# Experts that gather rows normalised but not yet scaled, with the norm's factor and addend applied at the transposed columns

## The chip, the cores and the metric

The kernel runs on one core of one Trainium2 chip. The metric is the device time of one execution in microseconds. Engines are named as in the profile: PE multiplies matrices, PEld is PE's queue of weight loads, DVE, ACT and POOL do elementwise work, SP issues most DMA transfers.

## What is computed

One encoder layer over 512 tokens of width 1024: a token mixer (neighbourhood attention and a bidirectional gated delta rule), a layer norm, a mixture of experts with 4 groups of 8, and a second layer norm.

```python
x = layer_norm(DEEPNORM_ALPHA * x + mix, ln1_g, ln1_b)        # ((x - mean) * rsqrt(var + eps)) * g + b
group_p, group_idx = lax.top_k(softmax(xt @ w_router_group + b_router_group), 1)
...
top_l, top_i = lax.top_k(sel, 2)                              # two experts inside the group
top_p = softmax(top_l) * group_p
...
hg, hu = split(einsum('nd,edf->nef', xt, w_expert_gate_up), 2)
hid = silu(hg) * hu * combine[:, :, None]
y = einsum('nef,efd->nd', hid, w_expert_down)
x = layer_norm(DEEPNORM_ALPHA * x + y, ln2_g, ln2_b)
```

All 512 tokens pass the first norm; each then goes to two of 32 experts.

## The kernel before

The program has two parts. In the first (all that runs through `emit`, line 447 in the profile) instructions are recorded, and a planner orders them: it goes through the ready instructions with estimated costs, takes those with the longest chain behind them first, and `plan.prio` adds to or takes from that rank. The planner sees the first part alone. In the second part (`tc.manual_schedule`) instructions stand on their engines in the order in which the code is written.

The first part ends with the mixer's output projection, the first norm and the router. The output rows lie in `xn`, four tiles of 128 tokens by 1024. The router's logits are computed from rows not yet normalised and mended with mean and factor (`cg`, `lg`), with the norm's factor multiplied into the router's weights (`wgb`). Beside them the norm is applied to `xn` in place, tile by tile in halves of 512 columns: a scaling, the product with `ln1_g`, the sum with `ln1_b`. The table `NORM1` names the engine of each of these three steps (V is DVE, G is POOL, S is ACT). The finished rows are stored to `x1d` in HBM, from where later pairs gather them. On SP's queue these four stores stand among the loads of the first twenty expert weight units (`first`, units 10 to 19 here). DVE then finds each token's group and experts (`arg_first`), PE ranks the tokens of each expert (`rk`), and DVE makes `SL`, each token's slot, and from it `oh`, a one-hot matrix that picks the first two experts' tokens. 18 products into `warm` keep PE at work meanwhile. Behind that come the combining weights (`vals`), and a few small steps for experts with more than 64 tokens (`more`, `moreT`, `pre`, `base`, `sx`, `we`, `nw`), among them a PE transpose of `more` and a PE product of its copy `moreT`.

The second part goes over 16 pairs of experts and a last round for overflowing tokens. Pair 0's rows come from `xn` by a one-hot product straight into the transposed form `xT` (lines 1675 to 1681: 1024 columns as eight blocks of 128, tokens of the pair along the free axis). All later pairs are gathered from `x1d` by an indirect DMA into `xg` (`gather`), and `turn` transposes them on PE in two halves and copies each half to `xT` on ACT. For each pair `up` multiplies `xT` with the gate and up weights, `act` makes `hid`, `hidden` transposes it, `down` multiplies with the down weights, `split` rounds the result into two parts, and `combine` adds it to the kept rows `xn`, eight pieces per pair, one pair later. The letters of `REST` give the order behind `up`: a `act`, t `turn`, p the list of the pair after next (`prep`: four products with `vals` and two ACT copies into `ic`; then `follow` starts the gather), h `hidden`, c a piece of `combine`, k and d, e the tail. PE results of h and p go to two halves of one PSUM tile, `tp`.

Of the kernel before, what the change touches and what calls it, by code (L numbers as in the profile page):

```python
# [9 lines left out]
F32 = mybir.dt.float32  # L10
FR = mybir.dt.float32r
F16 = mybir.dt.float16
I32 = mybir.dt.int32
AF = mybir.ActivationFunctionType
OP = mybir.AluOpType
# [4 lines left out]
NT = 4  # L20
KC = 8
# [49 lines left out]
NU = 20  # L71
# [10 lines left out]
REST = "attpchcccccccdke"  # L82
REST0 = "ahdektctp"

NORM1 = "VGV VGV VGV VGV VVG VVG SGV SVG".split()
NORM2 = "VSGG QD QSGG QPS QSGV QSGV QPS QD A B A B".split()


# [389 lines left out]
def encoder_block(ctx, tc, aps, out):  # L478
# [683 lines left out]
    def first(u, place=None):  # L1162
        W[u] = place.tile([128, 4, 512], F32, name="wu") if place else [gm_tile(F32, "wu") for _ in range(4)]
        yield lambda: load(Y, u, W[u])
# [82 lines left out]
    cgp = pmm.tile([128, 2, 36], F32, name="mm")  # L1247
    for k in range(KC):
        PE.matmul(cgp, one, wgb[:, k], start=k == 0, stop=k == KC - 1)
    cg = cp.tile([128, 2, 36], F32, name="cg")  # L1250
    V.tensor_copy(cg[:, 0], cgp[:, 0])
    V.tensor_tensor(cg[:, 1], cgp[:, 1], rb, op=OP.add)
# [57 lines left out]
            plan.prio = 0.0  # L1310
    wcs.close()
    wx.close()
    wc = pool("wc", NU - 14)
    for u in range(10, NU):
        for f in first(u, wc if u < NU - 4 else None):
            f()

    cq = pool("cq", 1, stack=pc)

# [11 lines left out]
    for t in range(NT):  # L1331
        v = xn[:, t]
        plan.prio = 20.0 if t == 3 else 0.0
        mv, r = norm_stats(ct, v)
        nm = ct.tile([128, 1], F32, name="nm")
        V.tensor_scalar(nm, mv[:, 0:1], -1.0, None, op0=OP.mult)
        plan.prio = 0.0
        V.scalar_tensor_tensor(lg[:, t], cg[:, 0], nm, lgp[t // 3][:, t % 3], op0=OP.mult, op1=OP.add)
        V.scalar_tensor_tensor(lg[:, t], lg[:, t], r, cg[:, 1], op0=OP.mult, op1=OP.add)
        plan.prio = 0.0  # L1340
        if "S" in NORM1[2 * t] + NORM1[2 * t + 1]:
            G.tensor_tensor(nm, nm, r, op=OP.mult)
        for h in range(2):
            c = v[:, h * 512:h * 512 + 512]
            g_, b_ = ln1[:, 0, h * 512:h * 512 + 512], ln1[:, 1, h * 512:h * 512 + 512]
            m = NORM1[2 * t + h]
            if m[0] == "S":
                S.activation(c, c, AF.Identity, scale=r, bias=nm)
            else:
                V.tensor_scalar(c, c, mv[:, 0:1], r, op0=OP.subtract, op1=OP.mult)  # L1350
            (V if m[1] == "V" else G).tensor_tensor(c, c, g_, op=OP.mult)
            (V if m[2] == "V" else G).tensor_tensor(c, c, b_, op=OP.add)
    for t in range(NT):
        Y.dma_start(x1d[t * 128:t * 128 + 128], xn[:, t])


    desc = C2["desc"]
# [1 line left out]
    def one_hot(oh, sl):  # L1359

        sh = [128, NT, 2, 64]
        V.tensor_tensor(oh.rearrange("p t (a s) -> p t a s", a=2),
                        C2["iota"][:, None, None, 0:64].to_broadcast(sh),
                        sl.unsqueeze(3).to_broadcast(sh), op=OP.is_equal)
# [45 lines left out]
    for i in range(18):  # L1410
        PE.matmul(warm[:, i % 4], ident, ew, start=True, stop=True, skip_group_check=True)

    plan.prio = -20.0
    ge = cq.tile(g4, F32, name="ge")
    V.tensor_tensor(ge, gl, gm.unsqueeze(2).to_broadcast(g4), op=OP.subtract)
    S.activation(ge, ge, AF.Exp)
# [26 lines left out]
    V.tensor_tensor(vals[:, :, :, 1], Cf, vals[:, :, :, 0].bitcast(F32), op=OP.subtract)  # L1443
    V.tensor_tensor(vals[:, :, :, 2].rearrange("p t (g e) -> p t g e", e=8), tk, ogb, op=OP.mult)

    ni = cq.tile([128, 32], I32, name="ni")
    V.tensor_scalar(ni, rk[:, 4], 1.0, -1.0, op0=OP.max, op1=OP.add)
    V.tensor_scalar(ni, ni, 6, None, op0=OP.logical_shift_right)
# [4 lines left out]
    G.affine_select(out=tri, in_=tri, pattern=[[1, 32]], compare_op=OP.is_ge, fill=0.0, base=0, channel_multiplier=-1)  # L1453
    mt = ppc.tile([128, 4, 128], F32, name="x1tp", bufs=2)
    PE.transpose(mt[0:32, 0], more, ident)
    moreT = cq.tile([32, 128], F32, name="moreT")
    V.tensor_copy(moreT, mt[0:32, 0])
    PE.matmul(mt[:, 1, 0:32], moreT, tri[0:32], start=True, stop=True, skip_group_check=True)
    pre = cq.tile([128, 32], F32, name="pre")
# [1 line left out]
    base = cq.tile([128, 32], F32, name="base")  # L1461
    V.tensor_tensor(base, pre, more, op=OP.subtract)
    V.tensor_scalar(base, base, 64.0, -64.0, op0=OP.mult, op1=OP.add)
    sx = cq.tile(s32, F32, name="sx")
    V.tensor_tensor(sx, SL, base[:, None].to_broadcast(s32), op=OP.add)
    V.scalar_tensor_tensor(sx, SL, 2048.0 + 64, sx, op0=OP.is_ge, op1=OP.mult)
    sm = mo.tile([128, 2, NT], F32, name="sm")
# [6 lines left out]
    for i, c in enumerate((c1, c2)):  # L1474
        V.tensor_copy(vm[:, i, :, 0], c)
        V.tensor_copy(vm[:, i, :, 2], C2["tokinv"])
    we = cq.tile([1, 16, 32], F32, name="we")
    V.tensor_scalar(pre, pre, 2048.0, None, op0=OP.add)
    V.tensor_tensor(we, C2["iota"][0:1, 0:16].unsqueeze(2).to_broadcast([1, 16, 32]),
                    pre[0:1, None].to_broadcast([1, 16, 32]), op=OP.is_ge)  # L1480
# [16 lines left out]
    def pool(name, bufs=1, space=None, stack=ctx, side=None):  # L1497
        kw = {} if space is None else {"space": space}
        if side is not None:
            kw["side"] = side  # L1500
        return stack.enter_context(tc.tile_pool(name=name, bufs=bufs, reuse_waits="tile", **kw))

    W = {u: [x.real() for x in w] if isinstance(w, list) else w.real() for u, w in W.items()}
    vals, SL, oh, nw, xn, sm, vm = [x.real() for x in (vals, SL, oh, nw, xn, sm, vm)]
    ident, magic = ident.real(), magic.real()
    C2 = {k: v.real() for k, v in C2.items()}
    ue = ExitStack()
# [41 lines left out]
        tc.chain_iter_dep(f"load{u % 2}", getattr(op[0], "ins", op[0]))  # L1549

    part = ep_.tile([128, 4, 512], FR, name="part", bufs=1)
    hot = ep_.tile([128, 512], FR, name="hot", bufs=1)
    xT = ep_.tile([128, KC, 128], F32, name="xT", bufs=1)
    xg = [ep_.tile([128, D], F32, name=f"xg{i}", bufs=1) for i in range(2)]
    for x in xg:
        G.memset(x, 0.0)
# [1 line left out]
    def turn(src, i, dst):  # L1558

        tp = pg.tile([128, 4, 128], F32, name="gat")  # L1560
        for k in range(4):
            PE.transpose(tp[:, k], src[:, (4 * i + k) * 128:(4 * i + k) * 128 + 128], ident)
        S.copy(dst[:, 4 * i:4 * i + 4], tp)

    def prep(ic, oh, e, ip):

        for t in range(NT):
            PE.matmul(ip[:, 0:6], oh[:, t], vals[:, t, e:e + 2].rearrange("p a b -> p (a b)"), start=t == 0,
                      stop=t == NT - 1, skip_group_check=True)
        for a in range(2):  # L1570
            S.copy(ic[rows2[a]], ip[rows2[a], 3 * a:3 * a + 3])  # L1571
# [53 lines left out]
    def small(j):  # L1625
        ic[j] = ep_.tile([128, 3], F32, name="ic", bufs=3)
        ix[j] = ep_.tile([128, 1], I32, name="ix", bufs=3)
        cw[j] = ep_.tile([128, 1], F32, name="cw", bufs=3)

    def follow(j, dst):  # L1630

        number(ic[j], ix[j])
        G.tensor_tensor(cw[j], ic[j][:, 0:1], ic[j][:, 1:2], op=OP.add)  # L1633
        if dst is not None:
            gather(ix[j], dst)
# [35 lines left out]
    with tc.manual_schedule():  # L1671
        experts = windows_experts()
        oh1 = hot.rearrange("p (t s) -> p t s", t=NT)
        one_hot(oh1, SL[:, :, 2:4])
        for i in range(2):
            gp_ = pg.tile([128, 4, 128], F32, name="gat")
            for k in range(4):
                for t in range(NT):
                    PE.matmul(gp_[:, k], xn[:, t, (4 * i + k) * 128:(4 * i + k) * 128 + 128], oh[:, t].bitcast(F32),
                              start=t == 0, stop=t == NT - 1, skip_group_check=True)  # L1680
            (S.copy if i == 0 else V.tensor_copy)(xT[:, 4 * i:4 * i + 4], gp_)
            if i == 0:
                ip = pu.tile([128, 2, 256], F32, name="tp", bufs=1)
                for j, o in ((1, oh1), (0, oh)):
                    small(j)
                    prep(ic[j], o, 2 * j, ip[:, 1, 8 * j:8 * j + 6])
                    follow(j, xg[1] if j else None)
        for j in range(NP + 1):
            here, there = xg[j % 2], xg[(j + 1) % 2]
            hp, tpi, yps, hid = tiles()  # L1690
# [265 lines left out]
```

## Time and profile before

| | |
|---|---|
| median of three runs | 911.08 us (908.28 to 913.6) |
| the profiled execution | 910.17 us, of it 908.5 us from first to last instruction |
| PE busy | 857.5 us (94%) |
| PEld busy | 598.8 us (66%) |
| DVE busy | 520.2 us (57%) |
| POOL busy | 363.6 us (40%) |
| ACT busy | 354.0 us (39%) |
| mean granted TensorE clock | 0.975 |

Busy shares are means over stages that have different limits. The mixer runs to about 575 us, the norm and the router to 605, the experts to about 882, the second norm to the end. A row of the timeline gives start, duration, engine, line, operation, output<-inputs, shapes and count; a square bracket at its end gives how long the engine had been idle and what released it. Instructions that the planner ordered all have line 447 and are told apart by their tiles. Rows of several instructions run from the start of the first to the end of the last.

### The profile page before, as it was taken

To read this page: it belongs to the slowest core of one execution; us is meant where nothing else is said; L and a number is where in the kernel's file an instruction comes from. 1 tells how busy PE (TensorE), PEld (TensorE's weight loads), DVE (VectorE), ACT (ScalarE), POOL (GpSimd) and SP (SyncE) were. 2 spreads that over 40 slices of the span, in tenths; PEclk is the share of its full clock that TensorE was granted. 3 is DMA by queue.
4 is the path that set the end of the run, shared out by engine and by line. 5 is a ranking of instruction groups with operands and counts; after the bars stand their busy time and mean duration, and the time that the engine had idled before them with its cause. 6 is when DMAs were issued, how large, how long until landed. Compare 5 with 4: busy or idle time off the path is not lost. (4 is left out here: it accounts for less than half of the span.)

```text
span 908.5 us, 15388 instructions
## 1 busy us (share of the span) xinstructions
PE 857.5 (94%) x5667; PEld 598.8 (66%) x5667; DVE 520.2 (57%) x1181; ACT 354.0 (39%) x925; POOL 363.6 (40%) x500
## 2 busy tenths in 40 slices
PE   7999999999999998999999999778999999999984
PEld 5786677778767777778788899754454444544441
DVE  6787889642526483831523537844556464564648
ACT  5465555542666765542443331102121111212114
POOL 5766567547737463636557741411010010100003
PEclk9998999999999997999999999799999999999997
DMA  6221101111312111011347275959998999998922
GB/s 246 89 85 47 48 24 48 48 47 48 113 40 76 48 54 47 2 48 47 93 184 280 81 264 206 361 225 349 393 357 309 333 363 340 353 384 308 371 93 93
DMA packets 39966, 157.72 MB, mean 174 GB/s; under 512 B 5786, under 2 KB 6042, under 8 KB 29008
## 3 DMA queue, kind: packets, MB, share of 16 engines
q1 hardware_dynamic: 37584, 152.81, 46.4%
q0 software_dynamic: 2304, 3.90, 1.2%
q8 instruction: 45, 0.74, 0.3%
q14 instruction: 33, 0.27, 0.1%
HBM read 156.99 MB, written 4.19 MB: 177 GB/s over the span
## 5 line engine op out<-in xcount | busy, mean ns | idle before, releaser
L447 POOL TENSOR_TENSOR wlo<-wraw,whi 128x256 fp32r<-128x256 f32 (+1 forms) x220 | 165.6, 766 | 148.0 <-ACT whi L447 108.6
L447 PE MATMUL mm<-xhi,whi 128*128 128x512 f32 (+1 forms) x360 | 140.2, 416 | 7.7 <-ACT whi L447 4.8
L447 PE MATMUL mm<-xhi,wlo 128*128 128x512 f32 (+1 forms) x360 | 139.2, 411 | 0.0
L447 PE MATMUL mm<-xlo,whi 128*128 128x512 f32 (+1 forms) x360 | 138.0, 410 | 0.2 <-DVE xlo L447 0.2
L447 ACT CAST whi<-wraw 128x256 fp32r<-128x256 f32 (+1 forms) x228 | 88.1, 404 | 118.0 <-PE mm L447 73.5
L1647 PE MATMUL hp<-wu,xT 128*64 128x512 f32 x544 | 119.7, 592 | 0.0
L1633 POOL TENSOR_TENSOR cw<-ic 128x1 f32<-128x1 f32 x17 | 3.2, 186 | 220.5 <-ACT ic L1571 205.1
L1647 PEld LDWEIGHTS hp<-wu,xT 128*64 128x64 f32 x544 | 38.9, 137 | 76.7 <-issue 74.8
L447 PEld LDWEIGHTS mm<-xhi,whi 128*128 128x128 f32 (+1 forms) x360 | 67.7, 190 | 24.3 <-ACT whi L447 5.1
L1621 DVE TENSOR_TENSOR xn<-xn,gat 128x512 f32<-128x512 f32 x128 | 79.2, 681 | 3.9 <-PE gat L1619 3.9
L447 PEld LDWEIGHTS mm<-xlo,whi 128*128 128x128 f32 (+1 forms) x360 | 67.7, 190 | 12.1 <-DVE xlo L447 1.1
L447 PEld LDWEIGHTS mm<-xhi,wlo 128*128 128x128 f32 (+1 forms) x360 | 67.4, 190 | 11.1 <-POOL wlo L447 0.2
L1619 PE MATMUL gat<-part,hot 128*128 128x512 f32 x256 | 67.0, 404 | 0.0
L1668 PE MATMUL yp<-wu,hid 128*64 128x512 f32 x272 | 62.1, 598 | 0.5 <-ACT hid L1662 0.5
L1654 DVE SCALAR_TENSOR_TENSOR hid<-hid,hp 128x256 f32<-128x256 f32 x17 | 7.2, 421 | 91.9 <-ACT hid L1653 91.9
L1611 ACT CAST part<-yp 128x512 fp32r<-128x512 f32 x34 | 19.8, 586 | 95.2 <-PE yp L1668 94.0
L447 DVE TENSOR_TENSOR RR<-RR,ps 128x512 f16<-128x512 f16 x64 | 42.8, 682 | 17.6 <-PE ps L447 17.4
L1619 PEld LDWEIGHTS gat<-part,hot 128*128 128x128 f32 x256 | 45.4, 189 | 9.4 <-issue 0.8
L1653 ACT ACTIVATE hid<-hp 128x256 f32<-128x256 f32 x17 | 6.5, 384 | 110.2 <-PE hp L1647 110.2
L1668 PEld LDWEIGHTS yp<-wu,hid 128*64 128x64 f32 x272 | 18.0, 136 | 35.6 <-issue 34.9
L447 DVE TENSOR_TENSOR ylv<-ps,mlv 128x256 f16<-128x256 f32 x64 | 26.2, 419 | 18.8 <-PE ps L447 18.3
L447 PEld LDWEIGHTS <-RR 128*128 128x128 f16 x448 | 23.6, 100 | 16.2 <-issue 13.4
(375 smaller groups left out, 1763.0 us busy)
## 6 DMA issues: line engine op xcount, KB each, us to landing
wu<-in_wgu SPq DMA_DIRECT2D x54, 1024.0 KB, 6.6
wu<-in_wdn SPq DMA_DIRECT2D x28, 1024.0 KB, 6.7
wraw<-in_wT SPq DMA_DIRECT2D x42, 512.0 KB, 3.4
wu<-in_wgu SPq DMA_DIRECT2D x56, 256.0 KB, 5.7
wu<-in_wdn SPq DMA_DIRECT2D x24, 256.0 KB, 4.6
wraw<-in_wp SPq DMA_DIRECT2D x8, 512.0 KB, 3.7
wraw<-in_wo SPq DMA_DIRECT2D x8, 512.0 KB, 4.0
kqv<-in_rpb SPq DMA_DIRECT2D x4, 640.0 KB, 3.9
```

The costliest lines, as they stand in the source:

```text
L447: getattr(self.eng[o.eng], o.call)(*[f(v) for v in o.args], **{k: f(v) for k, v in o.kw.items()})
L1611: S.copy(part[:, c], yps[c])
L1619: PE.matmul(sm_, hot[:, t * 128:t * 128 + 128], part[:, 2 * i + h], start=i == 0, stop=i == 1)
L1621: V.tensor_tensor(v, v, sm_, op=OP.add)
L1633: G.tensor_tensor(cw[j], ic[j][:, 0:1], ic[j][:, 1:2], op=OP.add)
L1647: PE.matmul(hp[rows2[h]], xT[:, k, rows2[h]], gw(j, h, k), start=k == 0, stop=k == KC - 1, skip_group_check=True)
L1653: S.activation(hid, hp[:, 0:256], AF.Tanh, scale=0.5)
L1654: V.scalar_tensor_tensor(hid, hid, 1.0, hp[:, 0:256], op0=OP.add, op1=OP.mult)
L1668: PE.matmul(y[rows2[h]], hT[:, f, rows2[h]], dw(j, h, f, c), start=f == 0, stop=f == 1, skip_group_check=True)
```

## The change

Three things change. The first norm only scales the rows in place (`NORM1` now has one letter for each half: DVE for tokens 0 to 255, ACT for the others), and rows without `ln1_g` and `ln1_b` are stored and gathered. Where rows reach the transposed form `xT`, a column of the model lies on one partition, so factor and addend are one number each per partition: `gb` holds them, and the copies into `xT` become ACT activations of 128x128 with `scale` and `bias` from `gb`, four for each half instead of one copy of 512 columns. This holds for pair 0 and for `turn` in all later pairs. The kept rows `xn`, to which the experts' output is added, get factor and addend on DVE behind pair 0's gather: 16 products and sums of 128x512.

Pair 0's gather, `hot` and the one-hot of pair 1 move from the second part into the first, so that the planner orders them. The loads of units 14 to 19 are recorded behind the last store. Some small tiles (`moreT`, `sx`, `we`) reuse other tiles' memory.

```diff
-NORM1 = "VGV VGV VGV VGV VVG VVG SGV SVG".split()
+NORM1 = "V V V V S S S S".split()
...
+    gb = mo.tile([128, KC, 2], F32, name="gb")
+    V.tensor_copy(gb, wr[:, :, 36:38])
...
-    for u in range(10, NU):
-        for f in first(u, wc if u < NU - 4 else None):
-            f()
+    def fill(us):
+        for u in us:
+            for f in first(u, wc if u < NU - 4 else None):
+                f()
+
+    fill(range(10, 14))
...
             if m[0] == "S":
                 S.activation(c, c, AF.Identity, scale=r, bias=nm)
             else:
                 V.tensor_scalar(c, c, mv[:, 0:1], r, op0=OP.subtract, op1=OP.mult)
-            (V if m[1] == "V" else G).tensor_tensor(c, c, g_, op=OP.mult)
-            (V if m[2] == "V" else G).tensor_tensor(c, c, b_, op=OP.add)
     for t in range(NT):
-        Y.dma_start(x1d[t * 128:t * 128 + 128], xn[:, t])
+        stored = Y.dma_start(x1d[t * 128:t * 128 + 128], xn[:, t])
+    plan.behind = stored
+    fill(range(14, NU))
+    plan.behind = None
...
-    plan.prio = -20.0
+    xT = xtp.tile([128, KC, 128], F32, name="xT")
+    for i in range(2):
+        gp_ = ppc.tile([128, 4, 128], F32, name="x1tp", bufs=2)
+        for k in range(4):
+            for t in range(NT):
+                PE.matmul(gp_[:, k], xn[:, t, (4 * i + k) * 128:(4 * i + k) * 128 + 128], oh[:, t].bitcast(F32),
+                          start=t == 0, stop=t == NT - 1, skip_group_check=True)
+        for k in range(4 * i, 4 * i + 4):
+            S.activation(xT[:, k], gp_[:, k % 4], AF.Identity, scale=gb[:, k, 0:1], bias=gb[:, k, 1:2])
+    plan.prio = -10.0
+    for h in range(2):
+        for t in range(NT):
+            c = xn[:, t, h * 512:h * 512 + 512]
+            for i in range(2):
+                V.tensor_tensor(c, c, ln1[:, i, h * 512:h * 512 + 512], op=OP.add if i else OP.mult)
+
+    plan.prio = 3.0
+    hot = xtp.tile([128, 512], FR, name="hot")
+    one_hot(hot.rearrange("p (t s) -> p t s", t=NT), SL[:, :, 2:4])
...
+    plan.prio = -20.0
     ni = cq.tile([128, 32], I32, name="ni")
...
-    moreT = cq.tile([32, 128], F32, name="moreT")
+    moreT = ct.tile([128, 4, 128], F32, name="x1T")[0:32, 0]
...
-        S.copy(dst[:, 4 * i:4 * i + 4], tp)
+        for k in range(4 * i, 4 * i + 4):
+            S.activation(dst[:, k], tp[:, k % 4], AF.Identity, scale=gb[:, k, 0:1], bias=gb[:, k, 1:2])
...
-        one_hot(oh1, SL[:, :, 2:4])
-        for i in range(2):
-            gp_ = pg.tile([128, 4, 128], F32, name="gat")
-            for k in range(4):
-                for t in range(NT):
-                    PE.matmul(gp_[:, k], xn[:, t, (4 * i + k) * 128:(4 * i + k) * 128 + 128], oh[:, t].bitcast(F32),
-                              start=t == 0, stop=t == NT - 1, skip_group_check=True)
-            (S.copy if i == 0 else V.tensor_copy)(xT[:, 4 * i:4 * i + 4], gp_)
-            if i == 0:
-                ip = pu.tile([128, 2, 256], F32, name="tp", bufs=1)
-                for j, o in ((1, oh1), (0, oh)):
-                    small(j)
-                    prep(ic[j], o, 2 * j, ip[:, 1, 8 * j:8 * j + 6])
-                    follow(j, xg[1] if j else None)
+        ip = pu.tile([128, 2, 256], F32, name="tp", bufs=1)
+        for j, o in ((1, oh1), (0, oh)):
+            small(j)
+            prep(ic[j], o, 2 * j, ip[:, 1, 8 * j:8 * j + 6])
+            follow(j, xg[1] if j else None)
```

What stands on an engine in a row now differs at three places. First ACT in one of the pairs, before:

```order
L1563 COPY xT<-gat 128x512 x2
L1571 COPY ic<-tp 64x3 x2
L1662 COPY hid<-tp 128x256
L1611 CAST part<-yp_8169 128x512
L1611 CAST part<-yp_8170 128x512
```

and the same place now:

```order
L1588 ACTIVATE xT<-gat,gb 128x128 x8
L1596 COPY ic<-tp 64x3 x2
L1687 COPY hid<-tp 128x256
L1636 CAST part<-yp_8198 128x512
L1636 CAST part<-yp_8199 128x512
```

Eight activations stand ahead of the two `ic` copies where two copies stood; PE's order in a pair is the same. Second, PE from the router's end to the first expert products, before (`x1tp<-tri,moreT` is the product of `moreT`, `gat<-oh,xn` is half of pair 0's gather, `tp<-vals` are the lists of pairs 1 and 0, `hp<-wu,xT` is `up` of pair 0):

```order
L447 MATMUL x1tp<-tri,moreT 128x32
L1679 MATMUL gat<-oh,xn 128x128 x16
L1568 MATMUL tp<-vals,hot 128x6 x4
L1568 MATMUL tp<-vals,oh 128x6 x4
L1679 MATMUL gat<-oh,xn 128x128 x16
L1647 MATMUL hp<-wu,xT 64x512 x16
```

and now (`mm<-s` is the last product of the ranks, `x1tp<-ao,con` are the last five warming products, of which 13 stand ahead of the ranks, and `x1T` in `x1tp<-tri,x1T` is `moreT` in its new memory):

```order
L447 MATMUL mm<-s_7527,mk_7525 128x32
L447 MATMUL x1tp<-ao,con 128x128 x5
L447 MATMUL x1tp<-oh,xn 128x128 x32
L447 MATMUL x1tp<-con,more 32x128
L447 MATMUL x1tp<-tri,x1T 128x32
L1593 MATMUL tp<-vals,hot 128x6 x4
L1593 MATMUL tp<-vals,oh 128x6 x4
L1672 MATMUL hp<-wu,xT 64x512 x16
```

The whole gather has moved ahead of the product of `moreT`, which still stands ahead of the lists and of `up`. Third, DVE behind `oh`, before:

```order
L447 TENSOR_TENSOR oh<-con,SL 128x512
L447 TENSOR_SCALAR ni<-ni 128x32
L447 RECIPROCAL c_7560<-c_7560 128x4
L447 CAST more<-ni 128x32
L447 SCALAR_TENSOR_TENSOR c_7560<-c_7560,gs 128x4
L447 TENSOR_TENSOR c_7563<-c_7560,ex 128x4
L447 TENSOR_TENSOR Cm<-ao,c_7560 128x128
L447 COPY moreT<-x1tp 32x128
```

and now, the last rows ahead of that copy (`xn<-xn,ln` are the kept rows' products and sums):

```order
L447 CAST vals<-Cm 128x128
L447 TENSOR_SCALAR ni<-mm 128x32
L447 TENSOR_TENSOR vals<-Cm,vals 128x128
L447 TENSOR_SCALAR ni<-ni 128x32
L447 TENSOR_TENSOR vals<-os,go 128x128
L447 CAST more<-ni 128x32
L447 COPY vm<-c_7542 128x4
L447 COPY vm<-c_7546 128x4
L447 COPY vm<-con 128x4 x2
L447 TENSOR_TENSOR xn<-xn,ln_6895 128x512 x16
L447 COPY x1T<-x1tp 32x128
```

The copy that PE's product of `moreT` needs now stands behind all 16 of them.

## Rows read from the trace of the kernel before

**Rows 1.** Stretch table: length; busy us (instructions) of PE, PEld, DVE, ACT, POOL; clock; DMA.

```profile
637.70:848.00 210.30, 209.96 (x1028) 100.63 (x1026) 115.46 (x222) 41.63 (x103) 15.44 (x26) 1.00 0.95 351
```

**Rows 2.** Timeline of one pair from its turn on: start us, duration us, engine, instruction.

```profile
644.68 1.09 PE L1562 MATMUL gat<-con,xg 128*128 128x128 f32 x8
...
645.37 1.07 ACT L1563 COPY xT<-gat 128x512 f32<-128x512 f32 x2
...
646.33 0.33 ACT L1571 COPY ic<-tp 64x3 f32<-64x3 f32 x2
...
646.71 0.20 PEld L1660 LDWEIGHTS tp<-con,hid 128*128 128x128 f32 x2 [0.46 <-ACT ic L1571]
646.71 0.44 PE L1660 MATMUL tp<-con,hid 128*128 128x128 f32 x2
...
647.65 3.08 DVE L1621 TENSOR_TENSOR xn<-xn,gat 128x512 f32<-128x512 f32 x5 [0.21 <-PE gat L1619]
```

**Rows 3.** List of waits from 640 to 860 us: total us, times, longest.

```profile
PEld tp L1660 <- ACT ic L1571: 5.5, 12, 0.5
```

**Rows 4.** Timeline of the last pair with a turn, which makes no list.

```profile
854.97 1.09 PE L1562 MATMUL gat<-con,xg 128*128 128x128 f32 x8
...
856.10 0.48 DVE L1655 SCALAR_TENSOR_TENSOR hid<-hid,cw,hp 128x256 f32<-128x256 f32 x1
...
856.73 0.41 PE L1660 MATMUL tp<-con,hid 128*128 128x128 f32 x2 [0.19 <-DVE hid L1655]
```

**Rows 5.** Timeline of DVE at the end of the router.

```profile
580.70 0.54 DVE L447 TENSOR_SCALAR xn<-xn,mv,ln_h 128x512 f32<-128x512 f32 x1
...
589.21 1.77 DVE L447 TENSOR_TENSOR xn<-xn,ln 128x512 f32<-128x512 f32 x1
...
591.22 0.29 DVE L447 TENSOR_TENSOR os<-ao,bo 128x128 f32<-128x128 f32 x1
591.43 0.17 DVE L447 TENSOR_TENSOR dm<-dm,go 128x16 f32<-128x16 f32 x1
591.55 0.29 DVE L447 TENSOR_TENSOR s<-os,go 128x128 f16<-128x128 f32 x1
...
593.08 0.69 DVE L447 TENSOR_TENSOR oh<-con,SL 128x512 fp32r<-128x512 f32 x1
```

**Rows 6.** Timeline of PE from the router to the first pair's expert matmuls.

```profile
584.24 6.93 PE L447 MATMUL x1tp<-ao,con 128*128 128x128 f32 x36 [4.96 <-DVE gw L447]
...
600.07 0.58 PE L1568 MATMUL tp<-vals,hot 128*128 128x6 f32 x4 [0.96 <-DVE hot L1583]
...
601.57 3.82 PE L1679 MATMUL gat<-oh,xn 128*128 128x128 f32 x32
...
605.32 7.09 PE L1647 MATMUL hp<-wu,xT 128*64 128x512 f32 x32
```

**Rows 7.** Stretch table around PE's pause in the router.

```profile
579.70:584.20 4.50, 0.00 (x0) 0.00 (x0) 4.50 (x22) 1.52 (x2) 1.60 (x2) 0.50 1.00 421
584.20:589.80 5.60, 5.56 (x26) 5.59 (x27) 5.60 (x10) 0.00 (x0) 3.69 (x3) 0.50 1.02 424
589.90:605.30 15.40, 10.97 (x101) 10.15 (x99) 10.21 (x50) 1.52 (x7) 4.02 (x7) 1.00 0.70 275
605.30:637.70 32.40, 28.65 (x141) 12.51 (x142) 12.71 (x26) 5.72 (x15) 2.39 (x4) 1.00 0.82 301
```

**Rows 8.** Timeline of ACT in the mixer.

```profile
59.12 1.16 ACT L447 ACTIVATE E<-psp,lb 128x128 f32<-128x128 f32 x4
```

**Rows 9.** Groups of ACT by shape: count, busy us, mean ns of one, idle before.

```profile
L447 ACT ACTIVATE E<-psp,lb 128x128 f32<-128x128 f32 x64 | 18.2, 370 | 11.5 <-PE psp L447 11.4
L1563 ACT COPY xT<-gat 128x512 f32<-128x512 f32 x32 | 17.2, 589 | 7.7 <-PE gat L1562 6.2
...
L447 ACT ACTIVATE xn<-ysum,nm,rs_y 128x512 f32<-128x512 f32 x3 | 2.2, 774 | 4.3 <-DVE nm L447 4.3
```

**Rows 10.** Timeline of PE ahead of the third pair's turn.

```profile
628.54 1.09 PE L1562 MATMUL gat<-con,xg 128*128 128x128 f32 x8 [1.55 <-DMA xg<-x1d,ix]
```

**Rows 11.** Timeline of PE at the turn of the pair behind rows 2.

```profile
660.74 1.09 PE L1562 MATMUL gat<-con,xg 128*128 128x128 f32 x8
```

More of the change, by code (lines that the diff above doesn't have):

```diff
@@ L1312, in encoder_block @@
     wx.close()
+    xtp = pool("xtp", 1)
     wc = pool("wc", NU - 14)
-    for u in range(10, NU):
-        for f in first(u, wc if u < NU - 4 else None):
-            f()
+    def fill(us):
[3 more added lines that the diff above has]
+    fill(range(10, 14))
     cq = pool("cq", 1, stack=pc)
@@ L1344, in encoder_block @@
             c = v[:, h * 512:h * 512 + 512]
-            g_, b_ = ln1[:, 0, h * 512:h * 512 + 512], ln1[:, 1, h * 512:h * 512 + 512]
             m = NORM1[2 * t + h]
@@ L1463, in encoder_block @@
     V.tensor_scalar(base, base, 64.0, -64.0, op0=OP.mult, op1=OP.add)
-    sx = cq.tile(s32, F32, name="sx")
+    sx = o2.rearrange("p t g e -> p t (g e)")
     V.tensor_tensor(sx, SL, base[:, None].to_broadcast(s32), op=OP.add)
@@ L1476, in encoder_block @@
         V.tensor_copy(vm[:, i, :, 2], C2["tokinv"])
-    we = cq.tile([1, 16, 32], F32, name="we")
+    we = ct.tile([128, 4, 128], F32, name="x1T").rearrange("p a b -> p (a b)")[0:1].rearrange("p (a b) -> p a b", b=32)
     V.tensor_scalar(pre, pre, 2048.0, None, op0=OP.add)
@@ L1503, in encoder_block @@
     W = {u: [x.real() for x in w] if isinstance(w, list) else w.real() for u, w in W.items()}
-    vals, SL, oh, nw, xn, sm, vm = [x.real() for x in (vals, SL, oh, nw, xn, sm, vm)]
+    vals, SL, oh, nw, xn, sm, vm, xT, gb, hot = [x.real() for x in (vals, SL, oh, nw, xn, sm, vm, xT, gb, hot)]
     ident, magic = ident.real(), magic.real()
@@ L1551, in encoder_block @@
     part = ep_.tile([128, 4, 512], FR, name="part", bufs=1)
-    hot = ep_.tile([128, 512], FR, name="hot", bufs=1)
-    xT = ep_.tile([128, KC, 128], F32, name="xT", bufs=1)
     xg = [ep_.tile([128, D], F32, name=f"xg{i}", bufs=1) for i in range(2)]
```

## The prediction, made before the changed kernel was run

> **What bounds the kernel now.** I read the table of stretches first. Between 637.7 and 848.0 us, where the experts run pair by pair, PE is busy 209.96 of 210.30 us at the full clock, and ACT only 41.6 [rows 1]. PE's queue is the bound there, so whatever makes PE stand still once per pair is paid some fifteen times. The reader should not take ACT's low share for slack: what counts is where in a pair PE waits for ACT.
>
> For that I read one pair instruction by instruction [rows 2]. PE turns the gathered rows (L1562, 644.68). ACT copies the two halves out into `xT` (L1563, 645.37, two copies in 1.07 us), then copies the pair-after-next's list `ic` (L1571, 646.33, done 646.66). PE's next step, the transposes of `hid` (L1660), starts at 646.71, 0.05 us behind that copy, and the load queue gives `ACT ic` as what ended its wait. `hid` and the list share the PSUM tile `tp`, and so does the wait. The list of waits has it 12 times in this stretch [rows 3]. A pair without a list shows the other bound: its `hid` transposes stand 1.76 us behind the turn (854.97 to 856.73) instead of 2.03, and follow DVE's `hid` (856.10 + 0.48), not ACT [rows 4]. So ACT's chain from turn to `ic` already ends last in a pair, by 0.27 us, and any length added to it is added to the pair.
>
> Last I read the router's end. DVE's chain from the last scalings (580.70) to `s` (591.55) holds sums and products of the norm, and beside POOL one of them takes 1.77 us [rows 5]. PE waits, is warmed with 18 products, gathers the first pair's rows and starts its experts at 605.32 [rows 6].
>
> **The change, part by part.**
>
> Head, the router. The norm's eight DVE products and sums, its eight on POOL and two of the six DVE scalings leave the chain; ACT takes two more scalings, beside DVE. In [rows 5] neighbours of 128 columns start 0.21 us apart (`os` to `dm`) and small ones 0.12 (`dm` to `s`). Some 12 of the first and 10 of the second stand ahead of `s`: 3.7 us, from 580.7, where a scaling now begins that leaves DVE. `s` is then done near 584.7, not 591.84. PE doesn't follow at once: 13 of the 18 warming products now stand ahead of the rank's. They took 6.93 / 18 = 0.385 us each [rows 6], at the low clock [rows 7], so 5.0 us from about 582.4, where their input, 1.3 us into the chain, reaches PE: rank at 587.4. From `s` done (591.84) to `oh` done (593.08 + 0.69) the trace has 1.9 us, which puts the end of `oh` at 589.3 instead of 593.77. A gain of 4.5.
>
> Head, the gather. It moves ahead of the small products and takes twice 3.82 us [rows 6], from 589.4 to 597.1. Its copies become eight ACT pieces, hidden behind what follows. The 16 products and sums on the kept rows now stand on DVE ahead of the copy of `moreT`, and PE's matmul on `moreT` stands ahead of the lists and of the first expert matmul. The first kept-row product needs the thirteenth of the sixteen gather products of its half: 592.5. DVE's sums of that size come 0.60 us apart ((3.08 - 0.68) / 4, [rows 2]); POOL has nothing left to disturb them, so 16 end at 602.1 (beside POOL, at 1.77 each, at 620; nothing in the order puts it there). Then the copy and the matmul, about 0.3 each (`os` has 0.29 [rows 5]) and 0.8 with their handovers, and the two lists with ACT between them, 1.5 (600.07 to 601.57, [rows 6]): the first expert matmul at 604.4, against 605.32. Term: **-0.9**. What was saved ahead is given back, since the kept rows are behind the first pair's gather but not behind its experts.
>
> Head, the clock. PE now stands still from about 597.4 to 602.6. In the trace it stood still from 579.7 to 584.2 and the granted clock was 0.50, that is 1.2 of 2.4 GHz, through that stretch and through the 5.6 us of work behind it, and 1.00 only then [rows 7]. So the first pair's matmuls start at the low clock. Half of 5.6 us is 2.8; nothing if the clock holds. I take **+2.5**.
>
> The loads. The stores of normalised rows stand earlier on SP's queue and six prefetched units behind them; PE needs those for the third pair, 30 us later, and the stores land before DVE overwrites the rows. SP's two reads of `nw` wait for DVE until about 606, and the first reload waits for PE until 608 anyway. I cost these at nothing.
>
> Each pair, the turn. Two copies of 128x512 become eight activations of 128x128 with a factor and an addend per partition. No such row exists. The nearest: 128x128 from PSUM with one such operand, `E`, four in 1.16 us with a mean of 0.370, so 0.263 apart [rows 8, 9]; and 128x512 from PSUM with both, 0.774, against 0.589 for the plain copy [rows 9]: 0.093 for each operand. So 0.356 apart, and `ic` can start 8 x 0.356 = 2.85 us behind the first piece, not 0.96 (645.37 to 646.33, [rows 2]). That is **1.89 us later per pair**. Bounds: 0.263 apart gives 1.14; no overlap at all, 0.370 + 0.093, gives 2.74. `hid`'s transposes, DVE's `ix` and the eight sums behind it wait with PE, so nothing absorbs it. It counts in pairs 1 to 13, where a list stands behind the turn and ahead of `hid`: 13 x 1.89 = **24.6** (14.8 to 35.6).
>
> The Trainium skill ("ScalarE: Activation LUTs", section "What ACT_TABLE_LOAD costs") gives an activation 186 ns + 0.833 ns per column, 93 ns for each per-partition operand and an overlap of 93 ns. An estimate from that page is 0.386 us apart, 2.13 us per pair, and a sum of 941; the 93 ns per operand agree with [rows 9]. Its fixed part, paid eight times instead of twice, is the rule that speaks against this change.
>
> Pair 0 turns pair 1's rows behind its `hid`, and the next matmul needs only the first piece, so nothing there. But the list of pair 2 is 1.9 us later, and with it its gather, for which PE already waits 1.55 us [rows 10]: **+1.9**.
>
> **How the numbers follow.** -0.9 + 2.5 + 1.9 + 24.6 = 28.1. The profiled execution took 910.2 us, 0.1% under the median of three; on it the sum is **938 us**, 3% slower. About 0.5% (4.6 us) is what a measurement of this kernel can tell from no change.
>
> **The rivals.**
>
> *Transfers hide it.* If the weights, not PE, set the pace of a pair, the longer ACT chain costs nothing and the end stays: 909 (910.2 less the head's 0.9), and 906 if the head keeps its 4.5 instead. For it: DMA engines are 95% busy in the stretch, and at its mean of 351 GB/s [rows 1] a pair's six loads of 1.05 MB take 17.9 us, as much as a pair of 16.1 + 1.9. It decides from the point where the loads can't come in less than 18 us. Against it: PE misses 0.34 us in 210 [rows 1], so they do come in 16.1. Chance 0.06.
>
> *The clock falls in the loop.* PE would stand still 2.2 us in each pair (0.27 + 1.89). In the trace PE's 1.55 us ahead of a turn [rows 10] lie in a stretch at 1.00, and its 4.5 us in one at 0.50 [rows 7]; 2.2 lies between. A fall like that one, 5.6 us of work at half speed, costs 2.8: in five pairs 14, so 952; in all thirteen 36, so 975. The Trainium skill ("TensorE: Matmul & The Clock Gate", section "HAM oscillation — how this bites in real kernels") tells of a loop whose wait dropped the clock in every tile; by that the sum would be the 975. Chance 0.15 for some pairs, 0.03 for all.
>
> *The pieces are cheap or the head keeps more.* At 0.263 apart 928; with the clock unharmed at the head 2.5 less. Chance 0.13 for 924 to 932.
>
> The forecast itself, 932 to 945, gets 0.63. The range of 8 in 10 takes in the cheap pieces and the falls of up to five pairs: 924 to 954. Faster by over 0.5% 0.02, within 0.5% 0.04, slower 0.94.
>
> **What would show it.** In the changed profile: eight activations per turn with about 0.36 us between starts; PE's load queue waiting some 2 us in 12 or 13 pairs for `ACT ic` ahead of `hid`; turns 18.0 us apart instead of 16.1 (644.68 [rows 2] to 660.74 [rows 11]); `s` near 584.7; `oh` near 589; kept-row products of 0.6 us on DVE until 602; the first expert matmul near 604 at a granted clock of 0.50. The prediction is wrong if the pieces start under 0.25 us apart, if PE passes `hid` before `ic` is out, or if the granted clock shows falls inside the loop.

## The result, and the profile after

The changed kernel took 950.46 us (median of four, 944.93 to 954.56), the kernel before 912.34 beside it: a ratio of 1.0421, with a 95% interval of 1.0355 to 1.0488. It is some 38 us slower. The sum had said 28 (938 us, own range 932 to 945); the stated range, 924 to 954, holds the median.

The profiled execution took 954.56 us, 952.8 of it from first to last instruction. The rows below are of that execution. The page's busy times first:

```profile
PE 872.9 (92%) x5667; PEld 608.7 (64%) x5667; DVE 523.5 (55%) x1187; ACT 386.1 (41%) x1030; POOL 352.4 (37%) x493
```

ACT works 32 us more than before (354.0), and the mean granted clock is 0.956 instead of 0.975. Then the table of stretches (columns as in [rows 1]) from pair 2's turn to pair 15's, 13 pairs that each make a list:

```profile
637.95:880.57 242.62, 219.05 (x1014) 106.74 (x1014) 116.64 (x220) 64.63 (x181) 15.42 (x26) 0.95 0.94 344
```

In [rows 1] PE was busy all but 0.34 us and the granted clock 1.00. Now PE is idle for 23.6 us of 242.62 and the mean clock is 0.95. One pair, instruction by instruction, as in [rows 2]:

```profile
657.95 1.09 PE L1586 MATMUL gat<-con,xg 128*128 128x128 f32 x8
...
658.65 2.90 ACT L1588 ACTIVATE xT<-gat,gb 128x128 f32<-128x128 f32 x8
...
661.40 0.34 ACT L1596 COPY ic<-tp 64x3 f32<-64x3 f32 x2
...
661.79 0.44 PE L1685 MATMUL tp<-con,hid 128*128 128x128 f32 x2 [1.83 <-ACT ic L1596]
```

The eight activations start 0.344 us apart (661.40 - 658.65 = 2.75, over 8). The list's copies stand behind them, and `hid`'s transposes behind those: 3.84 us behind the turn where [rows 2] had 2.03. PE's own queue, which had no wait there, now waits 1.83 us. Before, its product ahead of the transposes ended at 646.69, 0.02 us before they began:

```profile
645.98 0.71 PE L1619 MATMUL gat<-part,hot 128*128 128x512 f32 x2
```

The list of waits from 640 to 895 us has it 13 times:

```profile
PE tp L1685 <- ACT ic L1596: 23.6, 13, 1.8
```

The turns of three pairs in a row show the second loss: 17.89 us from the first to the second, 19.46 from the second to the third.

```profile
657.95 1.09 PE L1586 MATMUL gat<-con,xg 128*128 128x128 f32 x8
...
675.84 1.09 PE L1586 MATMUL gat<-con,xg 128*128 128x128 f32 x8
...
695.30 1.09 PE L1586 MATMUL gat<-con,xg 128*128 128x128 f32 x8
```

The stretch table behind PE's pause in the first of these pairs, and behind the pause in the second:

```profile
661.79:666.00 4.21, 4.21 (x20) 3.04 (x22) 4.00 (x8) 0.37 (x1) 1.19 (x2) 1.00 0.95 329
679.60:681.00 1.40, 1.32 (x6) 1.13 (x7) 1.12 (x3) 0.39 (x2) 0.62 (x2) 0.82 0.98 294
681.00:683.00 2.00, 2.00 (x6) 1.51 (x6) 1.69 (x3) 0.00 (x0) 0.57 (x1) 0.50 0.99 337
683.00:685.00 2.00, 2.00 (x9) 1.36 (x9) 1.67 (x4) 0.00 (x0) 0.00 (x0) 0.77 1.08 424
```

The pause is the same 1.83 us in both. Behind one the clock stays at 1.00, behind the other it is 0.50 (1.2 of 2.4 GHz) for a while. Of the 13 pairs with a list, six have such a fall, as their lengths show: 20.0, 19.46, 19.46, 19.47, 19.48 and 19.47 us, against 17.9 in the other seven.

The first of the six, 20.0 us, has another cause. There PE waited 3.07 us for pair 2's rows ahead of the turn. PE's timeline of this pair, and the stretch table around its pause ahead of `hid`:

```profile
637.95 1.09 PE L1586 MATMUL gat<-con,xg 128*128 128x128 f32 x8 [3.07 <-DMA xg<-x1d,ix]
...
639.25 0.96 PE L1644 MATMUL gat<-part,hot 128*128 128x512 f32 x2
641.85 0.69 PE L1685 MATMUL tp<-con,hid 128*128 128x128 f32 x2 [1.63 <-ACT ic L1596]
```

```profile
639.50:640.20 0.70, 0.70 (x2) 0.03 (x1) 0.00 (x0) 0.70 (x4) 0.00 (x0) 0.52 1.09 328
640.20:641.85 1.65, 0.02 (x2) 0.00 (x1) 0.02 (x1) 1.58 (x7) 0.00 (x0) 0.50 0.88 273
```

The clock was down before the pause began. So five of the other twelve pairs have a fall behind the pause, and one fall stands behind the wait for rows. All this is counted in one execution; the four differ by 9.6 us and have mean clocks of 0.956 to 0.963, so the count may differ among them.

Last the head, PE's timeline from the ranks to pair 0's `up`, and DVE beside it:

```profile
592.64 0.50 PE L447 MATMUL mm<-s,mk 128*128 128x32 f16 x14
...
594.42 7.38 PE L447 MATMUL x1tp<-oh,xn 128*128 128x128 f32 x64
...
608.01 0.60 PE L447 MATMUL x1tp<-tri,x1T 32*128 32x32 f32 x2 [6.10 <-DVE x1T L447]
...
610.91 9.41 PE L1672 MATMUL hp<-wu,xT 128*64 128x512 f32 x32
```

```profile
597.82 9.86 DVE L447 TENSOR_TENSOR xn<-xn,ln 128x512 f32<-128x512 f32 x16 [1.54 <-PE x1tp L447]
607.59 0.27 DVE L447 COPY x1T<-x1tp 32x128 f32<-32x128 f32 x1
```

PE stands still 6.10 us behind the sixteen kept-row steps, and `up` then takes 9.41 us instead of 7.09 [rows 6].

Both profiles can be set against each other from one event that the change doesn't touch, ACT's last copy into `x1T` in the router, at 577.56 before and 582.77 after:

```profile
577.56 0.59 ACT L447 COPY x1T<-x1tp 128x512 f32<-128x512 f32 x1 [1.95 <-PE x1tp L447]
```

```profile
582.77 0.59 ACT L447 COPY x1T<-x1tp 128x512 f32<-128x512 f32 x1 [1.95 <-PE x1tp L447]
```

| stretch | before, us | after, us | difference |
|---|---|---|---|
| router's last `x1T` copy to pair 0's first expert matmul | 27.76 | 28.14 | +0.4 |
| to pair 1's turn | 13.19 | 15.52 | +2.3 |
| to pair 2's turn | 10.03 | 11.52 | +1.5 |
| thirteen pairs with a list | 209.28 | 242.62 | +33.3 |
| one pair with the last round's list | 17.15 | 17.72 | +0.6 |
| to the end | 53.53 | 54.51 | +1.0 |

That is +39.1. The 5.2 us ahead of the event are not the change's: the kernels run below share the changed kernel's first part up to there, or the one of before, and had the event anywhere from 573.6 to 578.1. The table's 39.1 and the ratio's 38 agree.

### The profile page after: what moved, and what is told of

Read it like the earlier page. It is cut to its first block, busy times and chain, and to the rows that moved or that the text cites. A ratio compares the mean times of both kernels' runs of the same rounds, so it can differ in the third digit from the quotient of the medians.

```text
span 952.8 us, 15492 instructions
## 1 busy us (share of the span) xinstructions
PE 872.9 (92%) x5667; PEld 608.7 (64%) x5667; DVE 523.5 (55%) x1187; ACT 386.1 (41%) x1030; POOL 352.4 (37%) x493
## 5 line engine op out<-in xcount | busy, mean ns | idle before, releaser
L1672 PE MATMUL hp<-wu,xT 128*64 128x512 f32 x544 | 122.0, 602 | 0.0
L1646 DVE TENSOR_TENSOR xn<-xn,gat 128x512 f32<-128x512 f32 x128 | 81.4, 683 | 7.9 <-PE gat L1644 7.5
L1644 PE MATMUL gat<-part,hot 128*128 128x512 f32 x256 | 77.3, 452 | 0.0
L1644 PEld LDWEIGHTS gat<-part,hot 128*128 128x128 f32 x256 | 52.7, 217 | 12.2 <-issue 0.8
L1588 ACT ACTIVATE xT<-gat,gb 128x128 f32<-128x128 f32 x128 | 46.4, 467 | 9.3 <-PE gat L1586 7.7
```

The lines of the kernel that those rows point to most:

```text
L1588: S.activation(dst[:, k], tp[:, k % 4], AF.Identity, scale=gb[:, k, 0:1], bias=gb[:, k, 1:2])
L1644: PE.matmul(sm_, hot[:, t * 128:t * 128 + 128], part[:, 2 * i + h], start=i == 0, stop=i == 1)
L1646: V.tensor_tensor(v, v, sm_, op=OP.add)
L1672: PE.matmul(hp[rows2[h]], xT[:, k, rows2[h]], gw(j, h, k), start=k == 0, stop=k == KC - 1, skip_group_check=True)
```

## The experiments

All medians below are beside runs of the kernel before on the same chip, at 913 to 914 us.

**The turn alone taken back.** Two plain copies per turn again, everything else as changed:

```diff
-        for k in range(4 * i, 4 * i + 4):
-            S.activation(dst[:, k], tp[:, k % 4], AF.Identity, scale=gb[:, k, 0:1], bias=gb[:, k, 1:2])
+        S.copy(dst[:, 4 * i:4 * i + 4], tp)
```

> The changed kernel with the turn's eight activations put back to two plain copies of 512 columns; factor and addend are left out for pairs 1 to 15, so those experts work on unscaled rows; all else as changed. Theory (in each of 13 pairs PE waits for the list's copies, which stand on ACT behind the eight pieces, and the pause lowers PE's clock in some pairs): the turn-to-turn time goes back from 17.9 or 19.5 us to 16.1, PE's wait ahead of hid's transposes from 1.83 us to under 0.1, no granted clock under 1.00 between the third and the last pair, and the median near 915 us (the head's share, some +3, stays). Rival (the loss comes from what else is new: the kept rows on DVE, the order of the loads): pairs stay at 17.9 us or more and the time above 930.

Measured: 913.3 us, ratio 1.0012 (0.9983 to 1.0041). Pairs take 16.1 us, PE's queue has no wait ahead of `hid`, and the clock is 1.00:

```profile
630.67:840.00 209.33, 208.84 (x1015) 99.36 (x1015) 114.68 (x221) 41.12 (x103) 15.44 (x26) 1.00 0.98 371
```

So the turn's pieces carry the whole loss but 2 or 3 us. From the event of the table to the end, this kernel's profile is 2.7 us longer than the one before (333.6 and 330.9), of it 2.1 in pair 0's `up` (9.19 us instead of 7.09), which begins at the low clock. The kept rows, the loads' new order and the moved gather together cost about that; the interval allows up to 3.7.

**PE's order.** The pieces stay; PE gets other work ahead of `hid`, and the list comes later:

```diff
-REST = "attpchcccccccdke"
+REST = "attcchcccpcccdke"
```

> The changed kernel with the eight activations left as they are, but PE's order in a pair changed: the letters behind up are a t t c c h c c c p c c c d k e, so that hid's transposes stand ahead of the list and seven pieces of combine stand where PE waited. Theory (only PE's place in the queue makes the longer ACT chain cost anything): PE's pause ahead of hid goes from 1.83 us to under 0.3, pairs to 16.1 to 16.4 us, no clock falls in the loop, median 914 to 920. Rival (ACT's chain itself, by xT or by hid's copy, which stand behind the pieces too, sets the pair): the pause moves to another place, pairs stay over 17 us and the time above 930.

Measured: 919.12 us, ratio 1.0063 (1.0028 to 1.0098). Pairs take 16.39 us and the clock is 1.00, except in the first pair with a list, behind a wait of 2.58 us for its rows:

```profile
635.00:638.00 3.00, 3.00 (x10) 2.41 (x9) 1.37 (x2) 2.93 (x9) 0.00 (x0) 0.50 0.97 336
```

So 1.5 of the 1.8 us per pair were PE's place in its queue, not ACT's work: ACT does the same work here. The remaining 0.29 us is no pause that PE's own row shows. The load queue's longest new wait for ACT (650 to 860 us) is at the list's products, which now stand behind `hid`'s copy, and that behind the pieces; that this is where the 0.29 us go is not shown:

```profile
PEld tp L1593 <- ACT hid L1687: 5.2, 12, 0.4
```

**The price of a piece.** In the kernel before, eight plain copies of 128 columns:

```diff
-        S.copy(dst[:, 4 * i:4 * i + 4], tp)
+        for k in range(4 * i, 4 * i + 4):
+            S.copy(dst[:, k], tp[:, k % 4])
```

> The kernel before with the turn's two copies of 512 columns replaced by eight plain copies of 128 columns, no operand from gb; rows are finished before the store as before. It measures the disputed cost by itself: how much of the eight pieces is their number, how much the factor and the addend. Theory (0.344 us from piece to piece in the changed kernel, of it 0.09 for each per-partition operand or less): 0.25 us apart, the list's copies 2.0 us behind the first piece instead of 0.96, pairs 17.1 us instead of 16.1, 925 to 930 us if the clock stays, a few us more if such a pause already lowers it. Rival (the two operands are most of a piece): 0.17 us apart, pairs 16.5, under 918.

Measured: 918.94 us, ratio 1.006 (1.0027 to 1.0092). One turn in this kernel's timeline:

```profile
668.46 1.45 ACT L1564 COPY xT<-gat 128x128 f32<-128x128 f32 x8
669.72 0.36 ACT L1572 COPY ic<-tp 64x3 f32<-64x3 f32 x2
...
670.14 0.44 PE L1661 MATMUL tp<-con,hid 128*128 128x128 f32 x2 [0.36 <-ACT ic L1572]
```

Plain pieces start (669.72 - 668.46) / 8 = 0.158 us apart. The theory's 0.25 was wrong. The rival had the spacing (0.17) and the pair (16.5; pairs take 16.4) right, and its "under 918" just missed. Of the 0.344 us between the changed kernel's pieces, 0.186 are the two operands, 0.093 each. Cutting the copies in eight costs 0.3 us per pair; reading factor and addend per partition costs the other 1.5.

**PE kept at work.** Seven spare products per pair where PE paused; the list is as late as before:

```diff
+        for i in range(extra):          # 7 for the first piece of a pair
+            PE.matmul(sm_, hot[:, t * 128:t * 128 + 128], part[:, h], start=True, stop=True)
```

> The changed kernel with seven extra products of 128x512 per pair on PE, put into the first combine piece's bank ahead of its own two products (which start the bank anew), so that PE works where it paused ahead of hid's transposes. The list still comes as late. Theory (the falls of the granted clock follow from PE's pause of 1.8 us in a pair): clock 1.00 throughout the loop, all pairs 17.9 us, none of 19.5 or 20, the median some 10 us under the changed kernel: near 940. Rival (the falls come from the load on the memory or from the work itself): pairs of 19.5 us stay as many, and the time stays near 950 or rises.

Measured: 944.29 us, ratio 1.0359 (1.0334 to 1.0385) against 1.0421. From pair 3's turn on all pairs with a list take 17.9 us, none 19.5:

```profile
674.70 0.44 PE L1687 MATMUL tp<-con,hid 128*128 128x128 f32 x2 [0.23 <-ACT ic L1596]
```

The list comes as late as in the changed kernel, so the pair is as long. But PE pauses 0.23 us instead of 1.83, and the falls behind it are gone. They come from the pause. The gain is 6 us rather than 10: pair 2's rows were 4.3 us late in the profiled execution (3.07 in the changed kernel), the pair behind that wait took 19.03 us, at a low clock with no pause ahead of `hid`, and the last round's pair pays for the spare products.

**Longer and shorter pauses.** Twelve activations per turn, and six (the last two pieces on DVE):

```diff
+        for k in range(4 * i, 4 * i + 2):        # twelve: two of each half once more
+            S.activation(dst[:, k], tp[:, k % 4], AF.Identity, scale=gb[:, k, 0:1], bias=gb[:, k, 1:2])
```

```diff
+            if k >= 6:                            # six: these two on DVE
+                V.tensor_scalar(dst[:, k], tp[:, k % 4], gb[:, k, 0:1], gb[:, k, 1:2], op0=OP.mult, op1=OP.add)
```

> The changed kernel with twelve activations per turn instead of eight (two of each half done twice with the same result). PE's pause ahead of hid grows by 4 x 0.344 = 1.38 us to 3.2 us. Theory (a longer pause drops the clock in more pairs): pairs of 19.3 us without and 20.8 us or more with a fall, falls in most or all pairs, 975 us (968 to 985). Rival (how often the clock falls doesn't hang on the pause's length): six falls as in the changed kernel, 950 + 18 = 968.

> The changed kernel with the last two of a turn's eight pieces on DVE, so that six stand on ACT ahead of the list's copies. PE's pause ahead of hid shrinks by 2 x 0.344 = 0.69 to 1.14 us. Theory (the pause is what each pair pays, and a shorter one drops the clock less often): pairs of 17.2 us, at most two falls, 930 us (927 to 934). Rival (falls come with any pause): six falls, 938 or more.

Measured: 982.7 us, ratio 1.0763 (1.0724 to 1.0802), and 933.72 us, ratio 1.0232 (1.0193 to 1.0271). `hid` in one pair of each, twelve first:

```profile
679.93 0.50 PE L1687 MATMUL tp<-con,hid 128*128 128x128 f32 x2 [3.22 <-ACT ic L1598]
```

```profile
669.19 0.44 PE L1688 MATMUL tp<-con,hid 128*128 128x128 f32 x2 [1.14 <-ACT ic L1599]
```

| PE's pause ahead of `hid`, us | kernel | turn to turn, us | pairs with a fall, without the first | first pair, us |
|---|---|---|---|---|
| 0.36 | eight plain pieces | 16.4 | none of 12 | 18.67 |
| 1.14 | six activations | 17.28 | none of 12 | 19.75 |
| 1.83 | eight (the change) | 17.9 or 19.5 | 5 of 12 | 20.0 |
| 3.22 | twelve | 20.5 to 22.1 | 12 of 12 (17.9 + 1.39 = 19.3 would be without) | 21.84 |

The first of these pairs stands behind another wait, for the third pair's rows, and in each of the four kernels the clock had fallen before PE's pause ahead of `hid`, where it had one. Over all kernels here, such waits of 1.43, 2.58, 2.67, 3.05, 3.07, 3.61 and 4.30 us were followed by a fall, and those of 1.02, 1.28 and 1.55 (the kernel before) were not. The pause ahead of `hid` is paid in full in each pair; the falls come on top, and more often with a longer pause. Each kernel's falls are counted in one execution.

**Pieces on two engines.** The new order, with the second half's four pieces on DVE:

```diff
+            if i == 1:
+                V.tensor_scalar(dst[:, k], tp[:, k % 4], gb[:, k, 0:1], gb[:, k, 1:2], op0=OP.mult, op1=OP.add)
```

> The changed kernel with PE's order in a pair as in the run with seven combine pieces behind the turn (t t c c h c c c p c c c d k e), and the second half's four pieces on DVE (one multiply and add with the two columns of gb each) instead of ACT. In the run with the new order alone pairs took 16.39 us, 0.29 more than before, in three short waits of PE's loads (0.43 for hid's copy, 0.24 for xT's pieces, 0.16). Theory (these waits are ACT's eight pieces once more, now in front of hid's copy): with four pieces on each engine they go, pairs 16.1 us, the median 13 x 0.29 = 4 us lower, 915 (913 to 917). Rival (DVE's pieces stand in front of combine's sums and hold these up, or something other than the pieces makes the waits): pairs 16.4 us or more, 918 or more.

Measured: 920.53 us, ratio 1.0075 (1.0052 to 1.0098), no better than the new order alone. Pairs take 16.52 us; the rival was right. The list of waits (660 to 860 us) has PE's loads now behind DVE's pieces and behind DVE's sums, which free the banks for `combine`:

```profile
PEld gat L1647 <- DVE xT L1591: 5.0, 12, 0.4
...
PEld gat L1647 <- DVE xn L1649: 3.6, 12, 0.3
```

The two engines' pieces in one turn:

```profile
695.93 1.50 ACT L1589 ACTIVATE xT<-gat,gb 128x128 f32<-128x128 f32 x4
...
696.79 1.36 DVE L1591 TENSOR_SCALAR xT<-gat,gb 128x128 f32<-128x128 f32 x4
```

**The head.** The same, with the kept rows behind `moreT`:

```diff
-    plan.prio = -10.0
+    plan.prio = -60.0
     for h in range(2):
         for t in range(NT):
             c = xn[:, t, h * 512:h * 512 + 512]
```

The rest of this edit sees to it that nothing else waits for the kept rows: `part` is allocated behind the lists and `xg`, indices of the first two lists are made on POOL, and a constant of the last norm is set on DVE.

> The run above, and in the head: the kept rows' products and sums go behind the copy of moreT on DVE where these conflict (seven of the sixteen stay ahead, while PE gathers), the first two lists' indices are made on POOL, and the memory that the kept rows' last step frees goes to part instead of the lists and the gather's buffers, so that neither waits for the kept rows. Theory (the head's loss is PE's pause behind the kept rows and the low clock that it leaves): the first expert matmul comes 22 to 24 us behind the router's last x1T copy instead of 28.1, pair 0's up takes 7.1 us instead of 9.4, and the time is 6 to 8 us under the run above: 908 (905 to 911). Rival (pair 1's rows come only when they came before, so PE waits for them at the turn): up starts earlier, the third turn does not, 913 or more.

Measured: 916.34 us, ratio 1.0025 (1.0001 to 1.005), 4 us under the run above and not 7. PE's timeline:

```profile
600.82 8.78 PE L1674 MATMUL hp<-wu,xT 128*64 128x512 f32 x32
...
628.43 1.44 PE L1585 MATMUL gat<-con,xg 128*128 128x128 f32 x8 [2.67 <-DMA xg<-x1d,ix]
```

`up` starts 22.69 us behind the router's last `x1T` copy (578.13), 5.1 earlier than in the run above, as expected. But it still takes 8.78 us: PE pauses 1.6 us in three pieces around the lists, and the clock falls behind them. And at pair 2's turn (the third turn of the expectation) PE waits 2.67 us (1.02 above) for pair 2's rows, whose gather starts only behind pair 0's turn, and the clock falls once more behind that wait (a pair of 17.46 us). The rival had the right mechanism one pair too early.

**Columns for two pairs only.** Pairs 2 to 15 gather finished rows from a second array `x1f`, stored once the kept rows are done, and their turns are plain copies; only pairs 0 and 1 take factor and addend at the columns:

```diff
+    for t in range(NT):
+        Y.dma_start(x1f[t * 128:t * 128 + 128], xn[:, t])
...
-REST0 = "ahdektctp"
+REST0 = "ahpdektct"
```

> Factor and addend at the columns for pairs 0 and 1 only: the kept rows, once finished, are stored to a second array, from which pairs 2 to 15 and the last round gather, and their turns are two plain copies of 512 columns again, with the letters behind up as in the kernel before. The head is that of the run with the kept rows behind moreT; in pair 0 the list of pair 2 moves ahead of the down products (letters a h p d e k t c t), so that its gather starts some 8 us earlier. Theory (the loss was the eight pieces in 13 pairs; the head alone gains once PE doesn't wait behind the kept rows): pairs 16.1 us, no pause ahead of hid, no wait at the third turn, first expert matmul 22.7 us behind the last x1T copy against 27.8 before, 3 to 5 us under the kernel before: 910 (908 to 912 where it has 914). Rival (the 2 MB more of stores take the loads' time, and PE waits for weights later in the loop): pairs over 16.1 us towards the end, 914 or more.

> The kernel before with the one step of the run above that has nothing to do with the change: in pair 0 the list of pair 2 ahead of the down products. Theory: the wait of 1.55 us at the third turn goes, minus what the list now costs ahead of the down products: 1 to 1.5 us under the kernel before, hardly more than can be measured. Rival (most of what the run above gains is this step): 3 us or more.

Measured: 909.9 us where the kernel before had 913.11, ratio 0.9976 (0.9949 to 1.0003). The control, `REST0` alone in the kernel before: 912.02, ratio 0.9995 (0.9967 to 1.0023), no difference that the interval shows: its third turn no longer waits, but pair 0 up to pair 1's turn takes 15.43 us instead of 13.19. In the kernel with the second array the first expert matmul stands 24.05 us behind the last `x1T` copy (22.7 expected, 27.76 before), and no turn waits for rows. Pairs are back at 16.1 us without a fall, and the stretch shows no lack of weights towards the end:

```profile
641.20:834.60 193.40, 193.10 (x938) 91.95 (x936) 106.55 (x205) 38.42 (x96) 14.23 (x24) 1.00 0.96 357
```

The median is 3 us under before, as expected; the interval just reaches 1, so a gain is likely and not shown beyond doubt. It is the only version of the change whose median came out under the kernel before.

## Why the prediction was right or wrong

**Direction and mechanism: right.** The prediction rested on one reading, that `hid`'s transposes wait for a list's copies that stand on ACT behind the turn. Taking the pieces back removed the loss, and moving PE's order, with ACT unchanged, removed most of it.

**The term per pair: 24.6 us, measured 23.4.** The pieces stood 0.344 us apart, not 0.356, so 1.80 us per pair instead of 1.89. The two parts hold separately too: 0.093 for an operand, and 0.158 for a plain piece, which is what 0.263 less one operand comes close to (0.170). My own expectation for plain pieces, 0.25, is 0.344 less one operand; there are two. The Trainium skill ("ScalarE: Activation LUTs", section "What ACT_TABLE_LOAD costs") gives 93 ns for each per-partition operand, and the runs agree. Its overlap of 93 ns between neighbours was too small here: a piece took 0.467 us in this profile and the next started after 0.344, an overlap of 123 ns, so its 0.386 lay further off than the rows did.

**The head's start: -0.9, measured +0.4.** Counted from the event of the table, the steps up to there came within 0.4 us: the ranks (587.4 + 5.2 = 592.6, measured 592.64), the gather's start (594.6 and 594.42), the kept rows' first step (597.7 and 597.82) and their end (607.3 and 607.68). The rest is the two lists with ACT between them, 2.37 us (608.54 to 610.91) for the 1.5 taken from the trace of before: their products ran at the low clock, 1.01 us each instead of 0.58 [rows 6], which the sum had charged to `up` alone. (The price of a warming product, 0.385 us, was read as one at the low clock, though the last 1.3 us of its row lie in the stretch at 1.00 [rows 7]; the thirteen took 4.88 us instead of 5.0.)

**The head's clock: +2.5, measured +2.3**, in pair 0's `up`.

**Pair 2's gather: +1.9, measured +1.5**, and a fall of the clock behind its wait that the sum did not have; it is counted in the next term.

**The loop's clock: the step that failed.** The sum put the clock in the loop at 1.00, and the prediction named falls inside the loop as a sign that it is wrong. They came in six pairs and cost 20.0 - 17.9 + 5 x 1.57 = 9.9 us in the profiled execution: 7.8 in the five pairs behind the pause ahead of `hid`, 2.1 in the first, behind the wait for pair 2's rows, whose clock the prediction did not consider. With the 9.9 the sum would have been 38.

The rival had the right mechanism for the five. That its example of five pairs met the count is luck, as nothing led to that number, and its 2.8 us for a fall was too much: it is half of the 5.6 us of work at the low clock in [rows 7], and a fall behind the pause cost 1.57. Its pause of 2.2 us was also too long. The 0.27 in it was read from a pair without a list; in a pair with one PE's own work ended at 646.69, so nothing stood idle ahead of 646.71, and the measured pause is 1.83. The stated range holds the median because it took in this rival; the forecast itself, 932 to 945, does not hold it.

The runs with other pauses show why the rows of before could not decide it: 1.14 us every pair drops nothing, 1.83 drops the clock in five pairs of twelve, 3.22 in all. The Trainium skill ("TensorE: Matmul & The Clock Gate", section "HAM oscillation — how this bites in real kernels") tells of a loop whose waits drop the clock; that holds here at 3.22 us in each pair, and at 1.83 in five pairs of twelve.

**Left out of the sum:** the last round's pair (+0.6) and the way to the end (+1.0).

**The rivals.** Transfers did not hide anything: with plain turns the pairs came back to 16.1 us at 371 GB/s, so the loads can keep that pace. Nor were the pieces cheap: 0.344 us apart, not 0.263. That the head's 4.5 us are given back behind the kept rows was right: with these moved, `up` started 5 us earlier.

What stays open is why the same pause of 1.83 us drops the clock in one pair and not in the next, and why a single wait of 1.43 us for rows did so in one kernel where 1.55 did not in another. The pairs with a fall mostly alternate with those without; no run here took that apart.

## What to carry to other kernels

An engine that is busy a fifth of the time can still set the pace: look for what stands behind its work in its own queue, and at who waits for that, before giving it more instructions. An operation on many rows that is paid once ahead of a loop should not be moved into the loop because it is cheaper per row there; here only the first two passes needed the shortcut. Where a change makes the matrix engine pause in every pass, count the pause, and then count a second time for the clock: here pauses of 1.14 us cost only themselves, and pauses of 1.83 us brought a fall in five pairs of twelve.

## What the runs showed of the hardware

- Two per-partition operands more than doubled the time from one 128-column ACT piece to the next, from 0.158 to 0.344 us.
- Pauses of PE of 1.83 us in a stream of otherwise gapless matmuls lowered the granted clock to 0.50 in five pairs of twelve, pauses of 1.14 us in none, pauses of 3.22 us in all. Filling the pause with spare products ended it. A fall behind 1.83 us cost 1.57 us.
- Single waits of PE of 2.58 us and more for gathered rows were each followed by a clock of 0.50, those of 1.02, 1.28 and 1.55 us by none; one of 1.43 us was.
- DVE took 1.36 us for four multiply-and-adds of 128x128 from PSUM with two per-partition operands, ACT 1.50 us for the other four of the turn.
